# A picked expert's gate placed behind the next dot product, and GpSimd's query-weight remainders in four pieces

## The chip, the cores and the metric

The kernel runs on one core of a Trainium2 chip. The metric is the device time of one execution in microseconds (us). The kernel before takes 1302.95 us, the median of three runs (1302.8, 1302.95 and 1305.87). The engines are PE (TensorE), PEld (its weight loads), DVE (VectorE), ACT (ScalarE), POOL (GpSimd) and SP (SyncE, which only issues transfers).

## The reference

One step of a hybrid decoder: 256 prompt tokens with 16 meta tokens ahead of them and 8 × 8 tokens of running sequences pass a mixer (convolution and state-space branches) and then a layer of product-key experts. The change touches only the second half. 320 tokens are computed there, with 16384 experts of width 1024:

```python
def peer_block(xb, w_q, keys, U, V):
    q = (xb @ w_q).reshape(T, PEER_HEADS, 2, D_KEY // 2)
    s = jnp.einsum('thcd,hckd->thck', q, keys)
    s1, i1 = lax.top_k(s[:, :, 0], PEER_TOPK)
    s2, i2 = lax.top_k(s[:, :, 1], PEER_TOPK)
    ...
    ids = i1[f // 16] * N_KEYS + i2[f % 16]
    g = jax.nn.softmax(sc, axis=-1)
    act = jax.nn.gelu(jnp.einsum('thkd,td->thk', U[ids], xb))
    w = g * act
    return jnp.einsum('thk,thkd->td', w, V[ids])
```

Each token picks 16 experts in each of 8 heads. An expert's row of U gives, by a dot product with the token, its activation; a Gelu and the softmax weight make the gate; the gate scales the expert's row of V, and the 128 scaled rows are summed.

## The kernel before

**Up to 534 us** runs the mixer. The change leaves it as it is.

**Query weights (534 to 612 us, with the last of their products beyond).** Sixteen weights of 128 columns (j = 0 to 15) are loaded by SP. Each is split in a high part `wh`, rounded by ScalarE, and a low part `wl`, the remainder, computed by GpSimd (`split`, L244). The three products ah·wh, al·wh and ah·wl are summed on TensorE (L176), ScalarE copies the result out (`qT`, L1185), and TensorE multiplies it with the keys (`psc`, L1189). DVE then finds the 16 best keys (`top16`). In the loop stand also the preparations of the experts: at j = 4 the tokens' inputs, at j = `EXTRA` − 4 and j = `EXTRA` those of eight tokens apart (`x2e`, `acce`; the transposes `px`). At j = 7 the first four heads of the first 128 tokens are through: `heads_tasks(0)` computes their expert numbers `gid`, and `ahead(0)` issues the first gathers.

**Two ways to an expert's sum.** 128 tokens, and eight more in a second table, are *gathered*: 136 columns of picks (`NCOL`), each a column of 128 picks, one for each partition. The other 184 tokens (`ND`) are *dense*: for all 16384 experts, in 128 blocks, TensorE multiplies a block of U with the tokens (u-blocks, L1411), ScalarE takes the Gelu into S (L1413), S is multiplied by a table of the picked weights (`g_step`, L1435 to L1450, 23 for each half of the experts), and TensorE multiplies with the blocks of V (v-blocks, L1513). A block is 512 KB (`eraw`), is issued by SP or, for every odd one, by ScalarE (L1394), and lies in a ring of eight buffers.

**A column** is four steps: GpSimd gathers 128 rows of U and V side by side, 1 MB (`wuv`, five buffers, L1143); DVE forms 128 dot products (L1299, into `scg`); ScalarE applies Gelu (L1301) and the softmax weight (L1304); DVE adds gate times V row to `ygat` or `acce` (L1309). `pick_row(n)` emits, in this order, the gather of column n + 3 (`DEEP` = 4, the row's own column counted), dot n, Gelu and gate of n, and sum n − 1. A gather also waits for the block that lies `LEAD` = 4 steps back at that time. After the 64th v-block the distance is `NEAR` = 2 in place of `DEEP`.

**What sets the order.** A `Feed` hands out rows, the remaining top-16 tasks and the g_steps evenly between blocks: 45 rows in 84 u-blocks, 26 in the next 44 (with 23 g_steps), 35 in 64 v-blocks (with 23 g_steps), and the rest in the 61 blocks up to block 126, after which `finish` ends the gathered tokens and `finish_dense` the dense ones. Within this a scheduler orders each engine's instructions; a dependency marked `NoSync` orders without a wait in the hardware, one marked `Sync` waits. Each engine works strictly in its order, its transfers' issues included.

Of the kernel before, what the change touches and what calls it, by code (L numbers as in the profile page):

```python
# [7 lines left out]
F32 = mybir.dt.float32  # L8
# [6 lines left out]
OP = mybir.AluOpType  # L15
AX = mybir.AxisListType

D = 1024
# [24 lines left out]
NPICK = 128  # L43
NCOL = NPICK + (NPICK // XQ if NX else 0)
XAT = 64
HG = 4
EXTRA = 7
LEAD = 4
GT = 8
NP = 2  # L50
# [14 lines left out]
LATE = 24  # L65
OH = 2
UV = 5
DEEP = 4
NEAR = 2
GLAG = 12  # L70
XRES = 104
# [87 lines left out]
def body(tc, ia, oa, stop=None):  # L159
    nc = tc.nc  # L160
    with ExitStack() as top:
# [77 lines left out]
            nc.vector.tensor_tensor(v, v, t, op=OP.mult)  # L239
            nc.vector.scalar_tensor_tensor(dst, v, 1.5, t, op0=OP.add, op1=OP.mult)  # L240

        def split(h, l, src, on_pool=False, on_dve=False):
            (nc.vector.tensor_copy if on_dve else nc.scalar.copy)(h, src)  # L243
            (nc.gpsimd if on_pool else nc.vector).tensor_tensor(l, src, h.bitcast(F32), op=OP.subtract)  # L244

        def stack3(dst, src, n, pool, tag):
            w_ = src.shape[-1]
# [19 lines left out]
        def weight(src, i):  # L267
            raw = wp.tile([128, KD, 128], F32, name="wraw", bufs=rb[0])
            nc.sync.dma_start(raw, src[i].rearrange("p (k m) -> p k m", m=128))
            h = wp.tile([128, KD, 128], F32R, name="wh", bufs=2)  # L270
            l = wp.tile([128, KD, 128], F32R, name="wl", bufs=2)
            nw[0] += 1
            f_ = lm[0]
            on_dve = int((nw[0] + 1) * f_) > int(nw[0] * f_)
            split(h, l, raw, on_pool=not on_dve, on_dve=lm[0] == 1)
            return h, l

        lm, nw = [LM[3]], [NW0]
# [135 lines left out]
        def project(i, xs_=xn, name="pj"):  # L414
            if ready:
                return ready.pop(0)
            w = weight(ia["w_in"], i)
            pf = ps.tile([128, PJ], F32, name=name, tag="pj", bufs=3)
            proj(pf[:, :T if xs_ is xn else T2], w, xs_)
            return pf  # L420
# [503 lines left out]
        for j in range(KD):  # L924
# [5 lines left out]
            for s in range(2):  # L930
                w = weight(ia["w_mo"], 2 * j + s)
                proj(p, w, lambda k: tuple(yg[4 * s + k // 2][c_][:, k % 2, :] for c_ in range(2)),
                     first=(s == 0), last=(s == 1))
# [3 lines left out]
        for j in range(KD):  # L937
            w = weight(ia["w_o"], j)
# [6 lines left out]
                                           op0=OP.mult, op1=OP.subtract)  # L945
# [19 lines left out]
        x2m = gp.tile([NGAT, D], F32, name="x2m")  # L965
        gid = gp.tile([128, NCOL], I32, name="gid")
        ggw = gp.tile([128, NCOL], F32, name="ggw")
        scg = gp.tile([128, NCOL], F32, name="scg")
# [7 lines left out]
        if NX:  # L976
            x2e = gp.tile([128, D], F32, name="x2e")
# [28 lines left out]
        def expert_inputs():  # L1006
            nc.scalar.activation(x2m, ygat, AF.Copy, scale=rsT[:, 0:1])
            nc.gpsimd.tensor_tensor(x2m, x2m, n2r, op=OP.mult)
            for k in range(KD):
                nc.scalar.activation(nd[:, k], xT[:, k, NGAT:NGAT + ND], AF.Copy, scale=V("n2", k))  # L1010
                if k % 2:
                    nk = nd[:, k - 1:k + 1]
                    nc.gpsimd.tensor_tensor(nk, nk, rs2[:, None, NGAT:NGAT + ND].to_broadcast([128, 2, ND]), op=OP.mult)
# [3 lines left out]
        def extra_copies():  # L1017
            E0 = NGAT + ND
            x_ = gp.tile([128, 2 * D], F32, name="wuv", bufs=UV)[:, :(KD + 1) * 128].rearrange("p (k c) -> p k c", c=128)
            xes.append(x_)  # L1020
            v_ = x_.rearrange("p k (q t) -> p k q t", t=NX)
            nc.vector.tensor_copy(v_[:, KD], rs2[:, None, E0:T2].to_broadcast([128, XQ, NX]))
            nc.vector.tensor_copy(v_[:, :KD], xT[:, :, None, E0:T2].to_broadcast([128, KD, XQ, NX]))

        def extra_tokens():
            nc.gpsimd.memset(acce, 0.0)
            xe = xes[0][:, KD]
            p = misc([128, 4], "prs")
            nc.tensor.matmul(p[:, 3:4], xe, ident[:, 0:1], start=True, stop=True)
            nc.scalar.copy(rsT[:, 3:4], p[:, 3:4])  # L1030
            for c_ in range(2):
                p = misc([128, 512], "px")
                cs = slice(c_ * 512, c_ * 512 + 512)
                for k in range(4):
                    nc.tensor.transpose(p[:, k * 128:(k + 1) * 128], xes[0][:, 4 * c_ + k], ident)
                nc.scalar.copy(acce[:NX, cs], p[:NX])
                nc.scalar.activation(x2e[:, cs], p, AF.Copy, scale=rsT[:, 3:4])
                nc.gpsimd.tensor_tensor(x2e[:, cs], x2e[:, cs], n2r[:, cs], op=OP.mult)
# [97 lines left out]
        COLS = list(range(XAT)) + list(range(NPICK, NCOL)) + list(range(XAT, NPICK))  # L1136
# [15 lines left out]
        def ahead(n):  # L1152
            for i_ in range(n, min(n + (DEEP if len(vstep) <= HB else NEAR), NCOL)):
                if i_ not in pend:
                    pend[i_] = gather(COLS[i_])
# [20 lines left out]
        for j in range(16):  # L1176
# [4 lines left out]
            w = weight(ia["w_q"], j)  # L1181
# [5 lines left out]
            for i, (t0, L) in enumerate(KTILES):  # L1187
                n, up = 2 * heads_of[i], 64 * (j // (2 * heads_of[i]))
                nc.tensor.matmul(p[:, i], qT[:, t0 - up:t0 - up + 128], keys[:, j, :], start=True, stop=True)  # L1189
                s_ = sall[i][:, j % n] if i else kp.tile([128, NK], F32, name="sco", bufs=9)  # L1190
                scored = nc.scalar.copy(s_[up:up + L], p[up:up + L, i]).ins.name
                if i == 0:
                    top16(sv[i], si[i], s_[:L], j)
            if j == 4:
                expert_inputs()
            if j == EXTRA - 4:
                extra_copies()
            if j == EXTRA:
                extra_tokens()
# [7 lines left out]
        parts = [(0, SA), (SA, SB), (SB, 128)]  # L1207
# [87 lines left out]
        def pick_dot(n):  # L1295
            ahead(n)
            c, u = COLS[n], pend[n]
            w = scg[:, c:c + 1]
            nc.vector.scalar_tensor_tensor(u[:, :D], u[:, :D], 1.0, x2m if c < NPICK else x2e,  # L1299
                                           op0=OP.mult, op1=OP.mult, accum_out=w)  # L1300
            i_ = nc.scalar.activation(w, w, AF.Gelu)  # L1301
            tc.add_manual_dep(i_.ins, scored, mybir.DependencyInfo(mybir.DependencyClass.NoSync,
                                                                   mybir.DependencyReason.DATA), reason="scores first")
            nc.scalar.activation(w, w, AF.Copy, scale=ggw[:, c:c + 1])  # L1304

        def pick_sum(n):
            c, u = COLS[n], pend.pop(n)
            a_ = ygat if c < NPICK else acce
            nc.vector.scalar_tensor_tensor(a_, u[:, D:], scg[:, c:c + 1], a_, op0=OP.mult, op1=OP.add)  # L1309

        def group_sum():
            for c_ in range(2):
                p = misc([128, 512], "pgo")
                cs = slice(c_ * 512, c_ * 512 + 512)
                after(nc.tensor.matmul(p[:NX], C(f"sel{NX}"), acce[:, cs], start=True, stop=True), vstep[-1])
                nc.scalar.copy(x2e[:NX, cs], p[:NX])

        def pick_row(n):
            if NX and n == XAT - 9:
                extra_columns()  # L1320
            if n < NCOL:
                pick_dot(n)
            if n:
                pick_sum(n - 1)
            if NX and n == NCOL - GLAG:
                group_sum()

        ops = [(2.6, lambda n=n: pick_row(n)) for n in range(NCOL + 1)]

        def take(n):  # L1330
            t = ops[:n]
# [317 lines left out]
```

## Time and profile before

| | us |
|---|---|
| median of the runs | 1302.95 |
| the profiled execution | 1309.37 |
| its span in the profile | 1307.6 |
| query weights, scores, first picks | 534 to 612 |
| u-blocks 0 to 83, with the columns from 644 on | 612 to 785 |
| u-blocks 84 to 127, with g_steps | 785 to 960 |
| v-blocks | 960 to 1294 |
| finish of the dense tokens | 1294.8 to the end |

The profiled execution lasts 6.4 us longer than the median of the runs, so times of the trace are compared with this execution, and the difference between two states of the kernel is carried over to the median. A busy share that belongs to the whole span says little here, since the stages have different limits; the tables by stage and the waits of each engine are the views to read. In a waits table a row reads: engine, tile and line that waited, what released it, us in total, times, longest.

### The profile page before, as it was taken

The numbers are of one execution on the slowest core, as the hardware profiler recorded it, in microseconds if no ns is written. First come the engines' busy times: TensorE is split into PE (matmuls) and PEld (weight loads), VectorE is DVE, ScalarE is ACT, GpSimd is POOL, SyncE is SP. The second block draws the span as 40 slices with busy tenths as digits, with TensorE's granted clock in tenths as the row PEclk, the third lists the DMA queues.
The fourth block names the chain that finished last, engine by engine and source line by source line (L and its number), as shares of the span: only waits on it lengthen the run. The fifth ranks groups of instructions, "written<-read, shape, count | busy, mean of one in ns | idle before, by whom it ended". The sixth has DMA issues, their size and how long they took to land.

```text
span 1307.6 us, 23843 instructions
## 1 busy us (share of the span) xinstructions
PE 1274.4 (97%) x9015; PEld 1224.2 (94%) x9015; DVE 966.3 (74%) x2240; ACT 525.5 (40%) x1395; POOL 587.1 (45%) x504
## 2 busy tenths in 40 slices
PE   9999999999989999999998999999999999999997
PEld 7899989999879999999998999989999999999997
DVE  7978779878887235649998967788787887544444
ACT  6688777888766444534222221122211110101102
POOL 2487777877774666854042222223323322122210
PEclk9899999999999999999999999999999999999999
DMA  6434453454433444765889999999999999999992
GB/s 249 151 128 175 169 190 134 154 186 164 150 127 136 145 146 147 255 235 206 331 328 415 416 413 415 414 412 409 415 415 415 414 415 415 387 416 415 413 412 104
DMA packets 85907, 373.80 MB, mean 286 GB/s; under 512 B 10000, under 2 KB 15376, under 8 KB 66208
## 3 DMA queue, kind: packets, MB, share of 16 engines
q1 hardware_dynamic: 48336, 166.82, 34.5%
q0 software_dynamic: 19584, 142.62, 26.7%
q10 hardware_dynamic: 17872, 62.84, 12.1%
q8 instruction: 71, 1.16, 0.4%
q14 instruction: 44, 0.36, 0.1%
HBM read 359.18 MB, written 13.06 MB: 285 GB/s over the span
## 4 chain that ended last, share of the span: by engine, by line
PE 73%; DVE 13%; DMA 10%; ACT 2%; POOL 1%; issue 1%; DVEq 0%; ACTq 0%; POOLq 0%
PE pj L176 30%; PE va L1513 24%; PE pj L1411 10%; DMA wuv<-in_peer_uv_dram,gid 9%; DVE ygat L1309 2%; DVE pcv L505 1%; PE pg L1439 1%; PE pst L176 1%; DVE wuv L1299 1%; PE pdec L176 1%; PE po L176 1%; PE py L176 1%; DMA eraw<-in_uT_dram 1%; PE pq L176 1%; DVE pj L519 1%
## 5 line engine op out<-in xcount | busy, mean ns | idle before, releaser
L1143 POOL DMA_INDIRECT wuv<-in_peer_uv_dram,gid x136 | 176.7, 1299 | 485.7 <-PE va L1513 127.6
L244 POOL TENSOR_TENSOR wl<-wraw,wh 128x1024 fp32r<-128x1024 f32 x112 | 270.1, 2414 | 126.3 <-ACT wh L243 65.8
L1513 PE MATMUL va<-S,eraw 128*128 128x184 f32 x2048 | 325.4, 320 | 0.0
L1513 PEld LDWEIGHTS va<-S,eraw 128*128 128x128 f32 x2048 | 318.9, 190 | 0.9 <-issue 0.9
L1411 PE MATMUL pj<-nd,eraw 128*128 128x184 f32 x1792 | 293.9, 323 | 10.4 <-DMA eraw<-in_uT_dram 7.2
L1411 PEld LDWEIGHTS pj<-nd,eraw 128*128 128x128 f32 x1792 | 281.9, 192 | 12.4 <-issue 8.2
L176 PE MATMUL pj<-ah,wh 128*128 128x336 f32 (+1 forms) x768 | 243.9, 328 | 0.4 <-ACT xnf L219 0.4
L176 PE MATMUL pj<-al,wh 128*128 128x336 f32 (+1 forms) x768 | 233.5, 317 | 0.0
L1309 DVE SCALAR_TENSOR_TENSOR ygat<-wuv,scg,ygat 128x1024 f32<-128x1024 f32 x128 | 163.8, 1280 | 92.2 <-ACT scg L1304 92.2
L1301 ACT ACTIVATE scg<-scg 128x1 f32<-128x1 f32 x136 | 27.2, 202 | 455.4 <-DVE wuv L1299 326.4
L1299 DVE SCALAR_TENSOR_TENSOR wuv<-wuv,x2m 128x1024 f32<-128x1024 f32 x128 | 156.1, 1220 | 52.7 <-DMA wuv<-in_peer_uv_dram,gid 52.4
L243 ACT CAST wh<-wraw 128x1024 fp32r<-128x1024 f32 x125 | 131.0, 1049 | 80.4 <-PE pj L176 47.7
L505 DVE SCALAR_TENSOR_TENSOR pcv<-ccat,vec,pcv 128x256 f32<-128x256 f32 x464 | 149.0, 381 | 17.1 <-ACT pcv L503 17.1
L176 PEld LDWEIGHTS pj<-ah,wh 128*128 128x128 f32 x768 | 146.6, 191 | 6.2 <-issue 2.0
L176 PEld LDWEIGHTS pj<-al,wh 128*128 128x128 f32 x768 | 146.3, 191 | 0.9
L176 PE MATMUL pj<-ah,wl 128*128 128x336 f32 (+1 forms) x768 | 136.3, 315 | 0.7 <-POOL wl L244 0.7
L176 PEld LDWEIGHTS pj<-ah,wl 128*128 128x128 f32 x768 | 120.0, 189 | 1.2 <-POOL wl L244 1.0
L1413 ACT ACTIVATE S<-pj 128x184 f32<-128x184 f32 x128 | 37.4, 314 | 79.2 <-PE pj L1411 79.0
L519 DVE SCALAR_TENSOR_TENSOR pj<-mcat,vec,pj 128x360 f32<-128x360 f32 x96 | 56.4, 589 | 0.0
L219 ACT ACT_TABLE_LOAD x38 | 48.8, 1283 | 0.6
L1450 DVE SCALAR_TENSOR_TENSOR S<-pg,S 128x232 f32<-128x232 f32 (+1 forms) x92 | 34.5, 417 | 12.7 <-PE pg L1439 12.7
L1304 ACT ACTIVATE scg<-scg,ggw 128x1 f32<-128x1 f32 x136 | 39.7, 294 | 4.5 <-ACT scg L1301 0.2
(386 smaller groups left out, 1700.6 us busy)
## 6 DMA issues: line engine op xcount, KB each, us to landing
wraw<-in_w_in_dram SPq DMA_DIRECT2D x80, 512.0 KB, 4.3
eraw<-in_vE_dram SPq DMA_DIRECT2D x64, 512.0 KB, 10.2
eraw<-in_vE_dram ACTq DMA_DIRECT2D x64, 512.0 KB, 10.1
eraw<-in_uT_dram SPq DMA_DIRECT2D x60, 512.0 KB, 9.9
eraw<-in_uT_dram ACTq DMA_DIRECT2D x52, 512.0 KB, 10.0
st<-in_state_dram SPq DMA_DIRECT2D x8, 1024.0 KB, 6.9
out_ssm_s_dram<-st SPq DMA_DIRECT2D x8, 1024.0 KB, 6.3
wraw<-in_w_mo_dram SPq DMA_DIRECT2D x16, 512.0 KB, 3.2
```

Source lines behind the costliest of these rows:

```text
L176: i_ = nc.tensor.matmul(*a_, **kw)
L219: i_ = nc.scalar.activation(out, in_, f, **kw)
L243: (nc.vector.tensor_copy if on_dve else nc.scalar.copy)(h, src)
L244: (nc.gpsimd if on_pool else nc.vector).tensor_tensor(l, src, h.bitcast(F32), op=OP.subtract)
L505: t = nc.vector.scalar_tensor_tensor(o, i_, wv, a_, op0=OP.mult, op1=OP.add)
L519: nc.vector.scalar_tensor_tensor(o, cat[:, w:w + n], wv, o, op0=OP.mult, op1=OP.add)
L1143: i_ = nc.gpsimd.indirect_dma_start(out=u, out_offset=None, in_=ia["peer_uv"], in_offset=bass.IndirectOffsetOnAxis(ap=gid[:, c:c + 1], axi ...
L1299: nc.vector.scalar_tensor_tensor(u[:, :D], u[:, :D], 1.0, x2m if c < NPICK else x2e, op0=OP.mult, op1=OP.mult, accum_out=w)
L1304: nc.scalar.activation(w, w, AF.Copy, scale=ggw[:, c:c + 1])
L1309: nc.vector.scalar_tensor_tensor(a_, u[:, D:], scg[:, c:c + 1], a_, op0=OP.mult, op1=OP.add)
L1411: i_ = nc.tensor.matmul(p[:, :ND], raw[:, k, :], nd[:, k, :], start=(k == 0), stop=(k == KD - 1))
L1513: i_ = nc.tensor.matmul(va[k // 2][:, k % 2], raw[:, k, :], Sv(b), start=(b == 0 and k % 2 == 0), stop=(b == 127), skip_group_check=True)
```

## The change

Four edits, three of them to the columns and the first picks:

- `pick_row(n)` now emits dot n, then Gelu and gate of column n − 1, then sum n − 2. The Gelu of n − 1 is ordered behind dot n by a `NoSync` dependency ("rank"). There is one row more (`NCOL` + 2).
- `DEEP` is 3 and not 4, so row n emits the gather of column n + 2.
- `EXTRA` is 5 and not 7: the copies for the eight tokens apart come at j = 1 and not 3, their transposes and products at j = 5 and not 7.
- GpSimd's low part of each of the sixteen query weights is computed in four instructions of 128 x 256 and not in one of 128 x 1024. Other weights are split as before.

```diff
--- before.py
+++ after.py
@@ -44,7 +44,7 @@
 NCOL = NPICK + (NPICK // XQ if NX else 0)
 XAT = 64
 HG = 4
-EXTRA = 7
+EXTRA = 5
 LEAD = 4
 GT = 8
 NP = 2
@@ -65,7 +65,7 @@
 LATE = 24
 OH = 2
 UV = 5
-DEEP = 4
+DEEP = 3
 NEAR = 2
 GLAG = 12
 XRES = 104
@@ -239,9 +239,13 @@
             nc.vector.tensor_tensor(v, v, t, op=OP.mult)
             nc.vector.scalar_tensor_tensor(dst, v, 1.5, t, op0=OP.add, op1=OP.mult)
 
-        def split(h, l, src, on_pool=False, on_dve=False):
+        def split(h, l, src, on_pool=False, on_dve=False, parts=1):
             (nc.vector.tensor_copy if on_dve else nc.scalar.copy)(h, src)
-            (nc.gpsimd if on_pool else nc.vector).tensor_tensor(l, src, h.bitcast(F32), op=OP.subtract)
+            n = src.shape[1]
+            m = n // parts if on_pool and len(src.shape) == 3 else n
+            for q in range(0, n, m):
+                (nc.gpsimd if on_pool else nc.vector).tensor_tensor(l[:, q:q + m], src[:, q:q + m],
+                                                                    h[:, q:q + m].bitcast(F32), op=OP.subtract)
 
         def stack3(dst, src, n, pool, tag):
             w_ = src.shape[-1]
@@ -272,7 +276,7 @@
             nw[0] += 1
             f_ = lm[0]
             on_dve = int((nw[0] + 1) * f_) > int(nw[0] * f_)
-            split(h, l, raw, on_pool=not on_dve, on_dve=lm[0] == 1)
+            split(h, l, raw, on_pool=not on_dve, on_dve=lm[0] == 1, parts=1 if lm[0] else 4)
             return h, l
 
         lm, nw = [LM[3]], [NW0]
@@ -1295,12 +1299,18 @@
         def pick_dot(n):
             ahead(n)
             c, u = COLS[n], pend[n]
+            i_ = nc.vector.scalar_tensor_tensor(u[:, :D], u[:, :D], 1.0, x2m if c < NPICK else x2e,
+                                                op0=OP.mult, op1=OP.mult, accum_out=scg[:, c:c + 1])
+            return i_.ins.name
+
+        def pick_gate(n, behind):
+            c = COLS[n]
             w = scg[:, c:c + 1]
-            nc.vector.scalar_tensor_tensor(u[:, :D], u[:, :D], 1.0, x2m if c < NPICK else x2e,
-                                           op0=OP.mult, op1=OP.mult, accum_out=w)
             i_ = nc.scalar.activation(w, w, AF.Gelu)
-            tc.add_manual_dep(i_.ins, scored, mybir.DependencyInfo(mybir.DependencyClass.NoSync,
-                                                                   mybir.DependencyReason.DATA), reason="scores first")
+            for name in (scored, behind):
+                if name:
+                    tc.add_manual_dep(i_.ins, name, mybir.DependencyInfo(mybir.DependencyClass.NoSync,
+                                                                         mybir.DependencyReason.DATA), reason="rank")
             nc.scalar.activation(w, w, AF.Copy, scale=ggw[:, c:c + 1])
 
         def pick_sum(n):
@@ -1318,14 +1328,15 @@
         def pick_row(n):
             if NX and n == XAT - 9:
                 extra_columns()
-            if n < NCOL:
-                pick_dot(n)
-            if n:
-                pick_sum(n - 1)
+            behind = pick_dot(n) if n < NCOL else None
+            if 0 < n <= NCOL:
+                pick_gate(n - 1, behind)
+            if n > 1:
+                pick_sum(n - 2)
             if NX and n == NCOL - GLAG:
                 group_sum()
 
-        ops = [(2.6, lambda n=n: pick_row(n)) for n in range(NCOL + 1)]
+        ops = [(2.6, lambda n=n: pick_row(n)) for n in range(NCOL + 2)]
 
         def take(n):
             t = ops[:n]
```

Most lines of the changed kernel have other numbers: L244 is L247, L1143 is L1147, L1189 is L1193, L1299 is L1302, L1301 is L1309, L1304 is L1314, L1309 is L1319, L1394 is L1405, L1411 is L1422, L1413 is L1424, L1439 is L1450, L1450 is L1461.

On DVE, among the u-blocks with g_steps, the rows of before are these (L1299 is a dot, L1309 a sum; the number behind `wuv` tells the columns apart):

```order
L1309 SCALAR_TENSOR_TENSOR ygat_6624<-wuv_8761,scg_6628,ygat_6624 128x1024
L1299 SCALAR_TENSOR_TENSOR wuv_8779,scg_6628<-wuv_8779,x2m_6625 128x1024
L1435 TENSOR_TENSOR oh_9316<-oh_9316,gT_6631 128x512 x2
L1309 SCALAR_TENSOR_TENSOR ygat_6624<-wuv_8779,scg_6628,ygat_6624 128x1024
L1299 SCALAR_TENSOR_TENSOR wuv_8797,scg_6628<-wuv_8797,x2m_6625 128x1024
L1309 SCALAR_TENSOR_TENSOR ygat_6624<-wuv_8797,scg_6628,ygat_6624 128x1024
L1299 SCALAR_TENSOR_TENSOR wuv_8815,scg_6628<-wuv_8815,x2m_6625 128x1024
```

And of the changed kernel, at a like place (L1302 is a dot, L1319 a sum):

```order
L1446 TENSOR_TENSOR oh_9509<-oh_9509,gT_6631 128x512 x2
L1302 SCALAR_TENSOR_TENSOR wuv_8876,scg_6628<-wuv_8876,x2m_6625 128x1024
L1319 SCALAR_TENSOR_TENSOR ygat_6624<-wuv_8858,scg_6628,ygat_6624 128x1024
L1302 SCALAR_TENSOR_TENSOR wuv_8936,scg_6628<-wuv_8936,x2m_6625 128x1024
L1319 SCALAR_TENSOR_TENSOR ygat_6624<-wuv_8876,scg_6628,ygat_6624 128x1024
L1461 SCALAR_TENSOR_TENSOR S0_7582<-pg_9460,S0_7582 128x29x8
```

The sum of a column stood right behind its own dot (column 8797), and now stands behind the dot of the next column (8876 behind 8936), so a column's buffer is held for one row more. This holds for the whole program.

On TensorE the scores of j = 7 for the first 128 tokens are what `gid` waits for last. The rows of before around them (`qT_6682` in the last row is that of j = 7; the other `psc` rows belong to its neighbours):

```order
L176 MATMUL pj<-ah,wl 128x320 x2
L1189 MATMUL psc<-keys,qT_6681 128x128
L1189 MATMUL psc<-keys,qT_6683 128x128
L176 MATMUL pj<-ah,wl 128x320 x6
L1189 MATMUL psc<-keys,qT_6681 128x128
L1189 MATMUL psc<-keys,qT_6682 128x128
```

And of the changed kernel (the first `qT_6682` is that of j = 7):

```order
L176 MATMUL pj<-ah,wh 128x320
L176 MATMUL pj<-al,wh 128x320
L176 MATMUL pj<-ah,wl 128x320 x8
L1193 MATMUL psc<-keys,qT_6682 128x128
L1193 MATMUL psc<-keys,qT_6681 128x128
L1193 MATMUL psc<-keys,qT_6682 128x128
L1193 MATMUL psc<-keys,qT_6681 128x128
```

Counted from the first query product, 264 products stood ahead of these scores and now 288 do, a whole weight's 24 more; the eight transposes `px` of the eight tokens apart stood behind them and now stand ahead. On DVE 63 instructions stood between these scores and `gid` and now 70 do, and between `gid` and the first sum 113 small instructions beside five dots and now 96 beside five.

On GpSimd the rows of before from the tokens' inputs to the gathers (L244 is a low part, L1038 the inputs of the eight tokens apart, L1143 the gathers):

```order
L1008 TENSOR_TENSOR x2m<-x2m,wuv 128x1024
L244 TENSOR_TENSOR wl<-wraw,wh 128x1024 x9
L1038 TENSOR_TENSOR x2e<-x2e,wuv 128x512 x2
L244 TENSOR_TENSOR wl<-wraw,wh 128x1024
L1143 DMA wuv<-in_peer_uv_dram,gid 128x2048 x136
```

And of the changed kernel:

```order
L1012 TENSOR_TENSOR x2m<-x2m,wuv 128x1024
L247 TENSOR_TENSOR wl<-wraw,wh 128x256 x28
L1042 TENSOR_TENSOR x2e<-x2e,wuv 128x512
L247 TENSOR_TENSOR wl<-wraw,wh 128x256 x4
L1042 TENSOR_TENSOR x2e<-x2e,wuv 128x512
L247 TENSOR_TENSOR wl<-wraw,wh 128x256 x12
L1147 DMA wuv<-in_peer_uv_dram,gid 128x2048 x136
```

A weight's low part is four rows where it was one, and the inputs of the eight tokens apart stand before the last four and three weights, where they stood before the last one.

## The prediction

> **What bounds the kernel now.** The page's first part, then the busy time by stage, then TensorE's waits. In a stage row stand its start and end, its length, the busy time of PE, PEld, DVE, ACT and POOL, TensorE's granted clock, the DMA share and GB/s.
>
> ```profile
> PE 1274.4 (97%) x9015; PEld 1224.2 (94%) x9015; DVE 966.3 (74%) x2240; ACT 525.5 (40%) x1395; POOL 587.1 (45%) x504
> ```
> ```profile
> 534.00:612.00 78.00, 76.97 (x531) 75.19 (x530) 51.38 (x206) 36.66 (x90) 46.38 (x24) 1.00 0.65 228
> 612.00:645.00 33.00, 33.00 (x220) 33.00 (x219) 32.33 (x183) 9.81 (x39) 4.18 (x5) 1.00 0.93 357
> 645.00:683.00 38.00, 37.86 (x244) 37.58 (x243) 38.00 (x117) 8.88 (x28) 15.30 (x10) 1.00 0.83 303
> 683.00:785.00 102.00, 94.98 (x613) 93.23 (x612) 85.84 (x206) 25.18 (x89) 28.49 (x23) 0.98 1.02 415
> 785.00:880.00 95.00, 88.63 (x698) 86.31 (x697) 75.54 (x133) 17.31 (x71) 23.77 (x20) 0.98 1.02 414
> 880.00:960.00 80.00, 80.00 (x636) 79.07 (x635) 66.07 (x119) 16.86 (x64) 28.17 (x18) 1.00 1.02 412
> 960.00:1120.00 160.00, 160.00 (x1313) 158.60 (x1312) 130.53 (x228) 17.19 (x69) 44.20 (x34) 1.00 1.02 415
> ```
> ```profile
> PE pj L1411 <- DMA eraw<-in_uT_dram: 7.2, 4, 3.3
> PE pj L1411 <- ACT scg L1301: 3.1, 1, 3.1
> PE pg L1439 <- DVE oh L1435: 2.6, 2, 2.2
> ```
>
> TensorE sets the time. Nothing that the change touches runs before 534 us. From 880 to 1120 TensorE is busy throughout, and nothing can be gained there. Between 683 and 880 it is idle for 102.00 − 94.98 + 95.00 − 88.63 = 13.4 us. That is the whole budget for a gain, with the clock of 0.98 beside it (0.02 × 197 = 3.9 us at most). The waits name 12.9 us of it. In the same stages DVE is busy 85.84 of 102 us, and the DMA engines move 415 GB/s at a share of 1.02, so they are full as well.
>
> The next rows are the timeline at the second wait (start, duration, engine and line; the bracket is the idle time before).
>
> ```profile
> 693.42 0.20 ACT L1301 ACTIVATE scg<-scg 128x1 f32<-128x1 f32 x1 [3.92 <-DVE wuv L1299]
> 693.77 0.34 ACTq L1394 DMA_DIRECT2D eraw<-in_uT_dram  x1
> 697.78 1.22 DVE L1299 SCALAR_TENSOR_TENSOR wuv<-wuv,x2m 128x1024 f32<-128x1024 f32 x1 [1.12 <-DMA wuv<-in_peer_uv_dram,gid]
> 699.04 0.20 ACT L1301 ACTIVATE scg<-scg 128x1 f32<-128x1 f32 x1 [4.57 <-DVE wuv L1299]
> 699.31 21.85 PE L1411 MATMUL pj<-nd,eraw 128*128 128x184 f32 x128 [3.08 <-ACT scg L1301]
> ```
>
> ScalarE works in order. The Gelu of a column stands in its queue right after the row's block, and waits there for a dot product that DVE has not begun, here because the gather has not landed (1.12 us). Behind it stand the eviction of a finished u-block (L1413), which TensorE needs for its PSUM, and the issue of every second block load. TensorE lost 3.08 us to the eviction. The loads are the second price:
>
> ```profile
> 681.18 0.20 ACT L1301 ACTIVATE scg<-scg 128x1 f32<-128x1 f32 x1 [2.20 <-DVE wuv L1299]
> 681.43 0.33 ACTq L1394 DMA_DIRECT2D eraw<-in_uT_dram  x1
> 691.00 5.22 PE L1411 MATMUL pj<-nd,eraw 128*128 128x184 f32 x32 [2.10 <-DMA eraw<-in_uT_dram]
> 733.63 0.20 ACT L1301 ACTIVATE scg<-scg 128x1 f32<-128x1 f32 x1 [5.70 <-DVE wuv L1299]
> 733.87 0.34 ACTq L1394 DMA_DIRECT2D eraw<-in_uT_dram  x1
> 743.57 0.71 PE L1411 MATMUL pj<-nd,eraw 128*128 128x184 f32 x3 [0.95 <-DMA eraw<-in_uT_dram]
> 791.29 9.04 SPq L1288 DMA_DIRECT2D xigd<-xig  x4
> 819.08 4.24 PE L1411 MATMUL pj<-nd,eraw 128*128 128x184 f32 x16 [3.26 <-DMA eraw<-in_uT_dram]
> ```
>
> Twice a load issued by ScalarE right after such a wait lands 9.6 and 9.7 us later, at the moment at which TensorE's wait ends. The last of the four waits, 3.26 us, comes after SP's queue was held for 9.04 us by other transfers; ScalarE has no part in it.
>
> **The gate behind the next dot.** These rows are ScalarE's waits between 680 and 880, VectorE's waits for the gate in the whole run, and the gathers from issue to landing.
>
> ```profile
> ACT scg L1301 <- DVE wuv L1299: 140.4, 41, 5.7
> DVE ygat L1309 <- ACT scg L1304: 92.2, 67, 6.1
> wuv<-in_peer_uv_dram,gid POOLq DMA_INDIRECT x136, 17.0
> ```
>
> After the change the Gelu of column n−1 is asked for when dot n is next on DVE, and its own dot was done a whole column earlier. It is kept behind dot n in the scheduler's order, which is no wait on DVE in the hardware, so it runs at once. Most of the 140.4 us of ScalarE's waiting goes. What TensorE has of that: the eviction stall, −3.1 us; and the load stalls at 691 and 743 and the third one of the four, together 7.2 − 3.3 = −3.9 us. The second is bounded by 0 (the DMA engines are full, and an earlier issue only queues longer) and by 3.9; I take 3.9, since the two rows show landing 9.6 to 9.7 us after issue in the full stage itself. The 3.3 us at 819 stays. No instruction is added on ScalarE; it has the same two per column, and it is busy only 25.18 of 102 us.
>
> DVE gains also: the sum no longer waits for the gate (92.2 us in 67 waits). DVE is not on TensorE's path in these stages but for 2.6 us, so its worth lies between 0 and 2.6; I take 0, because the two waits at pg are bursts of work on DVE, not gates.
>
> What is late next: the buffer of a column comes free one row later, and the gathers go out three columns ahead and not four. A gather also waits for a block four steps back. At 84/45 = 1.87 blocks per row, a gather before has 3 × 1.87 + 4 = 9.6 blocks from its release to its dot, and now 2 × 1.87 + 4 = 7.7 blocks. A block is 21.85/8 = 2.73 us, so that is 26 us before and 21 us now, against 17.0 us to landing. It still fits, with 4 us to spare where there were 9. One gather less in flight is 1.05 MB, which at 415 GB/s is 2.5 us of DMA time that the block loads have sooner. That makes between −2.5 us (all of it falls on stalled loads) and +6 us (the third rival); I take 0, nearest the landing time, as the load stalls are already counted as gone.
>
> The Trainium skill, "DMA: Bandwidth & Descriptors", section "Queues, rings and completion order", says that each DMA engine takes turns between the queues that have work, a packet at a time. By that rule the gathers' share does not depend on how many of them wait, as long as one does, and the 2.5 us would be nothing. No row of the trace splits the share by queue over so short a stretch, so I keep 0 by the rows alone.
>
> **The start of the columns.** The order of the change shows the scores that the first 64 picks wait for after 24 more products and 8 transposes on TensorE, and 7 more small instructions on DVE from there to the gather indices; but 17 fewer small instructions between the indices and the first sum. The rows: the time of the indices and of the first sum, one small instruction, and the instructions that GpSimd's low parts hold up. Of these there are four between 595 and 602; the first is gh, the last pab; together they take 7.36 us and in the same forms at 737 to 740 together 1.29.
>
> ```profile
> 610.81 0.18 DVE L1120 CAST gid<-idh 128x64 int32<-128x64 f32 x1
> 644.60 1.18 DVE ygat L1309
> L1050 DVE FIND_INDEX8 si<-sv,sall 128x8 uint32<-128x128 f32 x24 | 6.7, 284 | 0.0
> 595.95 1.95 DVE L1122 TENSOR_TENSOR gh<-cv 128x64 f32<-128x64 f32 x1
> 601.14 2.38 DVE L1086 TENSOR_TENSOR pab<-pab,plo 128x64 bf16<-128x64 bf16 x1
> 600.63 2.81 POOL L244 TENSOR_TENSOR wl<-wraw,wh 128x1024 fp32r<-128x1024 f32 x1
> 737.20 0.20 DVE L1122 TENSOR_TENSOR gh<-cv 128x64 f32<-128x64 f32 x1
> 739.93 0.22 DVE L1086 TENSOR_TENSOR pab<-pab,plo 128x64 bf16<-128x64 bf16 x1
> L674 POOL TENSOR_TENSOR st<-st,el 128x256 f32<-128x256 f32 x64 | 37.9, 630 | 0.0
> L244 POOL TENSOR_TENSOR wl<-wraw,wh 128x1024 fp32r<-128x1024 f32 x112 | 270.1, 2414 | 126.3 <-ACT wh L243 65.8
> ```
>
> A product takes 33.00/220 = 0.15 us, so TensorE brings those scores 32 × 0.15 = 4.8 us later, and DVE adds 7 × 0.284 = 2.0. A small DVE instruction that met a low part ended with it (601.14 + 2.38 beside 600.63 + 2.81). With quarters of 0.63 us it waits a quarter at most: the 7.36 − 1.29 = 6.1 us lost shrink to 4 × 0.63 = 2.5, a gain of 3.6. The Trainium skill, "SBUF — State Buffer", section "SBUF: two separate sides", calls this port pair an exclusive lock that GpSimd or DVE holds for a whole instruction; by that rule four quarters back to back could win the lock again each time, and the gain would lie anywhere between 0 and 6.1 us. The indices come 4.8 + 2.0 − 3.6 = 3.2 us later, the first sum 17 × 0.284 = 4.8 us sooner than that: 1.6 us sooner than before, bounds −4.1 and +2.0 by the port waits. TensorE is busy throughout 612 to 683 whatever the columns do, so this is worth only what the DMA engines are ahead by at 683, when they are at 303 to 357 GB/s and later full: 0 to −1.6. I take 0.
>
> GpSimd itself: 64 × 0.63 = 40.3 us for 16 × 2.41 = 38.6, so +1.7 us over a stage in which it is idle 78 − 46.38 = 31.6 us. Cost 0; without that cover, 1.7.
>
> **The end.** The last columns go by the 61 blocks after the 64th; there is one row more to hand out, and the finishing of the picked tokens follows the last sum.
>
> ```profile
> 1288.04 2.42 DVE L1507 SCALAR_TENSOR_TENSOR wraw<-x2e,frs,wuv 128x512 f32<-128x512 f32 x2
> 1294.76 0.32 ACT L1525 ACTIVATE sqd<-va 128x184 f32<-128x184 f32 x1 [6.66 <-PE va L1513]
> ```
>
> It ends at 1290.5, 4.3 us ahead of TensorE's last products. A column without the gate's wait comes sooner, if anything. Cost 0; a second dot's time, 1.2, would still fit.
>
> **Sum.** −3.1 − 3.9 = −7.0 us against the profiled execution, 1309.37 us with a span of 1307.6, so 1302.4. That execution is 6.4 us above the median; I take the difference over to the median: 1302.95 − 7.0 = 1296.0.
>
> **Rivals.** First, everything idle goes: the whole 13.4 us, so 1289.6, and 1285.7 with the clock. For it speaks that ScalarE's waits were at every second block; against it the stall behind SP's transfers and the two at pg. Second, the DMA engines are the bound: at 415 GB/s a load issued sooner lands no sooner, and only the gather less in flight helps, 1302.95 − 2.5 = 1300.5. For it speaks the share of 1.02 through all the stages, against it that TensorE runs without a wait from 880 on at the same share. Third, slower: the gather has 21 us, and where it takes longer than that, dot n stands waiting at the head of DVE's in-order queue, with sum n−1 and its buffer and the one-hot (oh) of the next g_step behind it, and TensorE waits at pg. One such wait shows in this run:
>
> ```profile
> 878.00 0.95 PE L1439 MATMUL pg<-oh 128*128 128x64 f16 x16 [2.20 <-DVE oh L1435]
> ```
>
> At 2.2 us apiece, five of the 46 g_steps (23 for each half of the experts) undo the gain and reach +0.3%, and six give 6 × 2.2 − 7.0 = +6.2, so 1309. It decides from a mean landing of about 21 us; the 17.0 shown speaks against it. Since fewer gathers share the engines, it should rather fall.
>
> **Chances.** The forecast (1293 to 1299) 0.43, all the idle time 0.13, the DMA engines as the bound 0.26, slower 0.18. A measurement of this kernel tells 0.3%, 3.9 us, from no change. So faster 0.56, the same 0.26, slower 0.18. The range leaves about a fourth of the first rival and a third of the third out: 1288 to 1309. It takes in the bounds above, −7.0 − 2.5 − 1.6 = −11 and +6.
>
> **What would show it.** Right: ScalarE's waits for the dot (L1301 before) fall to a few us, DVE's for the gate to none, TensorE has no wait on the gate's line, and 3 to 4 us for block loads, the one behind SP's transfers; the indices come at about 614 and the first sum at about 643; no small DVE instruction beside a low part takes over 0.9 us; the gathers land in 17 us or less. Wrong: DVE's waits for gathers (52 us in the run) grow, TensorE's waits at pg grow past 2.6 us, or the idle time between 683 and 880 stays near 13 us under other names.

## The result and the profile after

The changed kernel is slower: 1320.29 us median of four runs (1319.77 to 1323.95) against 1304.41 (1302.8 to 1307.79), a ratio of 1.0128 with a 95% interval of 1.0111 to 1.0145. The forecast was 1296.0, within 1288 to 1309. The profiled execution lasted 1320.37 us, its span is 1318.6, so 11.0 us over the span of before. That is less than the 15.9 us between the medians, because the profiled execution of before lies 5.0 us above its median and this one at it.

The stages of the changed kernel, in the columns of the table by stage shown above, and TensorE's waits from 540 us on:

```profile
683.00:785.00 102.00, 97.88 (x654) 95.85 (x653) 87.08 (x215) 25.16 (x86) 21.90 (x21) 1.00 1.02 414
785.00:880.00 95.00, 90.28 (x721) 88.64 (x720) 68.27 (x125) 16.99 (x64) 17.23 (x16) 0.96 0.98 380
880.00:960.00 80.00, 80.00 (x635) 79.00 (x634) 60.27 (x110) 14.78 (x56) 17.60 (x15) 1.00 0.99 383
960.00:1120.00 160.00, 160.00 (x1289) 158.78 (x1288) 120.39 (x212) 14.81 (x60) 31.52 (x31) 1.00 1.00 393
```
```profile
PE prd L1537 <- ACT sqd L1536: 21.0, 1, 21.0
PE pj L1422 <- DMA eraw<-in_uT_dram: 7.4, 4, 4.7
PE pj L1422 <- ACT S L1424: 1.4, 2, 1.0
```

A part of the gain that was forecast is there: between 683 and 880 TensorE is idle for 4.12 + 4.72 = 8.8 us where it was 13.4. What is new is one wait of 21.0 us at the very end, and DMA engines that move less between 785 and 1120 (380 to 393 GB/s for 412 to 415 before). The timeline at the end shows the wait:

```profile
1224.42 60.00 PE L1524 MATMUL va<-S,eraw 128*128 128x184 f32 x384
1296.23 2.68 DVE L1319 SCALAR_TENSOR_TENSOR ygat<-wuv,scg,ygat 128x1024 f32<-128x1024 f32 x2
1305.05 0.32 ACT L1536 ACTIVATE sqd<-va 128x184 f32<-128x184 f32 x1 [1.63 <-DVE wraw L1518]
1305.43 5.02 PE L1537 MATMUL prd<-sqd,cst 128*128 128x184 f32 x16 [21.00 <-ACT sqd L1536]
```

TensorE ends its last v-block at 1284.4. The last sum of the gathered tokens ends only at 1298.9, their finish stands behind it on DVE and ScalarE, and the finish of the dense tokens behind that. The same 384 products before:

```profile
1236.59 60.00 PE L1513 MATMUL va<-S,eraw 128*128 128x184 f32 x384
```

They ended at 1296.6, and ScalarE was waiting for them. So the end costs (1318.6 − 1284.4) − (1307.6 − 1296.6) = 23.2 us more, and TensorE's way to it is 12.2 us shorter. Of these 12.2 the mixer, which the change does not touch, has 4.3, by the same products in both executions:

```profile
508.82 1.33 PE L176 MATMUL pj<-mh,wl 128*128 128x320 f32 x8
```
```profile
504.52 1.33 PE L176 MATMUL pj<-mh,wl 128*128 128x320 f32 x8
```

The first row is before, the second after. That leaves 7.9 us of gain on TensorE's way, and 23.2 − 7.9 − 4.3 = 11.0, the difference of the spans. Without the mixer's 4.3 it would be 15.3, close to the 15.9 between the medians.

The columns were late. The next rows count the sums (L1309, L1319) by stage; the number behind DVE's busy time is their count. Before:

```profile
785.00:960.00 175.00, 46.21 (x37) 0.99 1.02 413
960.00:1120.00 160.00, 43.58 (x34) 1.00 1.02 415
1265.00:1300.00 35.00, 5.14 (x4) 1.00 0.48 191
```

After:

```profile
785.00:960.00 175.00, 39.12 (x32) 0.98 0.99 381
960.00:1120.00 160.00, 39.67 (x31) 1.00 1.00 393
1265.00:1300.00 35.00, 16.66 (x13) 0.83 0.84 338
```

There are eight sums fewer between 785 and 1120, and 13 after 1265 where there were 4. One column shows what it went through. Before, column 48, first GpSimd's row of its gather and of the gather five columns on, then DVE's dot and sum:

```profile
832.60 0.94 POOL L1143 DMA_INDIRECT wuv<-in_peer_uv_dram,gid  x1 [1.84 <-issue]
...
856.47 0.94 POOL L1143 DMA_INDIRECT wuv<-in_peer_uv_dram,gid  x1 [1.84 <-PE pj L1411]
```
```profile
852.59 1.22 DVE L1299 SCALAR_TENSOR_TENSOR wuv<-wuv,x2m 128x1024 f32<-128x1024 f32 x1
...
854.42 1.28 DVE L1309 SCALAR_TENSOR_TENSOR ygat<-wuv,scg,ygat 128x1024 f32<-128x1024 f32 x1 [0.60 <-ACT scg L1304]
```

After, column 52, the same rows, and ScalarE's at its Gelu:

```profile
866.40 0.94 POOL L1147 DMA_INDIRECT wuv<-in_peer_uv_dram,gid  x1 [1.93 <-DVE ygat L1319]
...
896.99 0.94 POOL L1147 DMA_INDIRECT wuv<-in_peer_uv_dram,gid  x1 [7.77 <-PE pg L1450]
```
```profile
884.32 1.22 DVE L1302 SCALAR_TENSOR_TENSOR wuv<-wuv,x2m 128x1024 f32<-128x1024 f32 x1
...
890.91 1.22 DVE L1302 SCALAR_TENSOR_TENSOR wuv<-wuv,x2m 128x1024 f32<-128x1024 f32 x1
...
894.95 1.28 DVE L1319 SCALAR_TENSOR_TENSOR ygat<-wuv,scg,ygat 128x1024 f32<-128x1024 f32 x1 [2.80 <-ACT scg L1314]
```
```profile
894.00 0.32 ACT L1424 ACTIVATE S<-pj 128x184 f32<-128x184 f32 x1 [2.58 <-PE pj L1422]
894.00 0.33 ACTq L1405 DMA_DIRECT2D eraw<-in_uT_dram  x1
894.38 0.20 ACT L1309 ACTIVATE scg<-scg 128x1 f32<-128x1 f32 x1
```

Before, the sum starts 1.8 us after the dot. After, the dot starts at 884.32, the next dot at 890.91, the Gelu behind an eviction at 894.38 and the sum at 894.95, 10.6 us after its dot. Only then is the buffer free, and the gather five columns on is issued 2.0 us later. The buffer was held for 28.6 us and not 21.8. With five buffers a column takes (hold + 2.0)/5. The means over columns 40 to 63, from the start of the gather to the start of the sum, are all worked out from the trace. The last column counts the sums that stand in DVE's order ahead of the end of the 24th g_step (the first among the v-blocks) and of the 46th, the last:

| kernel | buffers | tie | hold, us | (hold + 2.0)/buffers | measured, us per column | sums ahead of g_step 24 / 46 |
|---|---|---|---|---|---|---|
| before | 5 | no | 22.0 | 4.8 | 4.85 | 71 / 105 |
| changed | 5 | yes | 26.3 | 5.7 | 5.45 | 63 / 92 |
| before, four buffers (e7) | 4 | no | 20.7 | 5.7 | 5.68 | 62 / 90 |
| changed, room for six, five used (e5) | 5 | yes | 25.1 | 5.4 | 5.43 | 63 / 92 |
| changed, six buffers (e6) | 6 | yes | 26.0 | 4.7 | 4.66 | 71 / 103 |

The kernel before makes a sum every 4.7 us here (175 us for 37 sums), and in all five rows a gather goes out as soon as a buffer is free (2.0 us after the sum begins, 2.3 in e6), so even the kernel before ran at the edge of its buffers. While that is so, the rule and the measured time must agree, and differ only by where the stretch is cut: the rule says what a column takes, not why the hold is long.

The landings in the trace say more. In the changed kernel the 26.3 us are 9.8 from issue to landing, 9.0 in which the landed rows lie, and 7.5 from the dot to the sum. No dot of columns 40 to 95 starts less than 4.4 us after its rows have landed. Before, the dot of columns 40 to 63 follows the landing by 1.2 us on average (18 of the 24 landings are on record), and the sum follows the dot by 2.7. DVE's waits for gathers between 785 and 1120 us, before and then after:

```profile
DVE wuv L1299 <- DMA wuv<-in_peer_uv_dram,gid: 26.4, 26, 1.9
```
```profile
DVE wuv L1302 <- DMA wuv<-in_peer_uv_dram,gid: 2.6, 1, 2.6
```

So in this stretch of the changed kernel a gather that went out sooner would have brought no dot forward. The columns go at the pace of the built order, which is fixed before the kernel runs: by the 24th g_step eight sums, and by the last one thirteen, had been put behind where they stood before. The tie and the number of buffers act on that order, as the table shows. That the scheduler counts the hold of a buffer as the rule does is likely, and not shown.

### The profile page after: what moved, and what is told of

Read it like the earlier page. It is cut to its first block, busy times and chain, and to the rows that moved or that the text cites. A ratio compares the mean times of both kernels' runs of the same rounds, so it can differ in the third digit from the quotient of the medians.

```text
span 1318.6 us, 23876 instructions
## 1 busy us (share of the span) xinstructions
PE 1271.4 (96%) x9015; PEld 1222.8 (93%) x9015; DVE 956.1 (73%) x2240; ACT 527.4 (40%) x1395; POOL 571.8 (43%) x552
## 4 chain that ended last, share of the span: by engine, by line
PE 76%; DVE 10%; DMA 9%; ACT 2%; issue 1%; POOL 1%; ACTq 0%; DVEq 0%; SPq 0%; POOLq 0%
PE pj L176 31%; PE va L1524 23%; PE pj L1422 13%; DMA wuv<-in_peer_uv_dram,gid 5%; DMA eraw<-in_uT_dram 3%; DVE ygat L1319 2%; PE pg L1450 1%; PE pst L176 1%; DVE wuv L1302 1%; PE po L176 1%; PE pdec L176 1%; PE py L176 1%; DVE pcv L509 1%; DMA wdt<-in_w_dt_dram 1%; PE pq L176 1%
## 5 line engine op out<-in xcount | busy, mean ns | idle before, releaser
L1147 POOL DMA_INDIRECT wuv<-in_peer_uv_dram,gid x136 | 151.5, 1114 | 537.8 <-PE va L1524 212.8
L247 POOL TENSOR_TENSOR wl<-wraw,wh 128x1024 fp32r<-128x1024 f32 (+1 forms) x160 | 280.3, 1766 | 117.1 <-ACT wh L243 68.9
L1422 PE MATMUL pj<-nd,eraw 128*128 128x184 f32 x1792 | 293.6, 323 | 8.8 <-DMA eraw<-in_uT_dram 7.4
L1422 PEld LDWEIGHTS pj<-nd,eraw 128*128 128x128 f32 x1792 | 280.9, 191 | 10.7 <-issue 8.4
L1319 DVE SCALAR_TENSOR_TENSOR ygat<-wuv,scg,ygat 128x1024 f32<-128x1024 f32 x128 | 164.0, 1281 | 99.5 <-ACT scg L1314 99.2
L1302 DVE SCALAR_TENSOR_TENSOR wuv<-wuv,x2m 128x1024 f32<-128x1024 f32 x128 | 156.0, 1218 | 30.3 <-DMA wuv<-in_peer_uv_dram,gid 28.8
L1309 ACT ACTIVATE scg<-scg 128x1 f32<-128x1 f32 x136 | 26.9, 200 | 366.3 <-PE va L1524 198.6
L1424 ACT ACTIVATE S<-pj 128x184 f32<-128x184 f32 x128 | 39.2, 320 | 179.2 <-PE pj L1422 171.9
L1461 DVE SCALAR_TENSOR_TENSOR S<-pg,S 128x232 f32<-128x232 f32 (+1 forms) x92 | 34.7, 419 | 53.8 <-PE pg L1450 53.8
L1314 ACT ACTIVATE scg<-scg,ggw 128x1 f32<-128x1 f32 x136 | 39.8, 294 | 8.6 <-PE va L1524 4.4
```

The lines of the kernel that those rows point to most:

```text
L247: (nc.gpsimd if on_pool else nc.vector).tensor_tensor(l[:, q:q + m], src[:, q:q + m], h[:, q:q + m].bitcast(F32), op=OP.subtract)
L1147: i_ = nc.gpsimd.indirect_dma_start(out=u, out_offset=None, in_=ia["peer_uv"], in_offset=bass.IndirectOffsetOnAxis(ap=gid[:, c:c + 1], axi ...
L1302: i_ = nc.vector.scalar_tensor_tensor(u[:, :D], u[:, :D], 1.0, x2m if c < NPICK else x2e, op0=OP.mult, op1=OP.mult, accum_out=scg[:, c:c + 1])
L1422: i_ = nc.tensor.matmul(p[:, :ND], raw[:, k, :], nd[:, k, :], start=(k == 0), stop=(k == KD - 1))
```

## The experiments

The theories. **Q**: the Gelu's place behind block loads on ScalarE is the cause. **B**: the sum behind the next dot holds a buffer for one column more, and five buffers don't carry it. **D**: gathers three ahead are too late. **W**: the query weights' part is to blame.

**e1, the columns' part alone.**

```diff
-EXTRA = 5
+EXTRA = 7
-split(..., parts=1 if lm[0] else 4)
+split(..., parts=1)
```

> The changed kernel with the query weights' low parts whole again and EXTRA at 7: only the columns' new order is left, with the gathers three ahead. Theory Q (queue): tying a column's Gelu behind the next dot moves it behind more block loads in ScalarE's fixed order, 12 Gelus come after the last block load here (13 in the changed kernel, 2 in the one before), each column holds its buffer for about 28 us instead of 21, and the columns end after TensorE; so 1317 to 1322 us, with TensorE waiting some 20 us for the finish. Theory D (depth): the gathers are issued too late because they are three ahead and not four; the same 1317 to 1322. Theory W (query weights): the first picks are to blame; then this is 1300 to 1306.

Measured: 1325.97 us, ratio 1.016 (1.0126 to 1.0194), 4 us above the range expected; TensorE waits 21.2 us at the end. W falls. The loss is larger than that of the whole change.

**e2, the query weights' part alone** (on the kernel before: `EXTRA = 5`, low parts in four).

> The kernel before with the low parts in quarters and EXTRA at 5 alone. Theories Q and D: no column is later, so 1300 to 1305 us; the gather indices come 3 to 6 us earlier than in the kernel before, as in the profile of the changed kernel, and nothing ends later. Theory W: 1315 to 1321.

Measured: 1304.64, ratio 0.9992 (0.9973 to 1.001), no difference. The indices came at 610.33 with the mixer at the time of before, so half a microsecond earlier and not 3 to 6: that part of the expectation missed.

**e3, without the tie.**

```diff
-            for name in (scored, behind):
+            for name in (scored,):
```

> The changed kernel without the tie of the Gelu behind the next dot; the gathers stay three ahead, the sums are still asked for two rows later, the quarters stay. Theory Q: ScalarE's order is that of before again (one Gelu after the last block load), so 1298 to 1306 us, and ScalarE waits over 300 us for dots as before. Theory D: the distance is what counts, so 1315 to 1321.

Measured: 1301.82, ratio 0.9973 (0.9954 to 0.9992), if anything faster than before. D falls, and with it the sums asked for two rows later: without the tie there is no loss. One Gelu stands behind the last block load in ScalarE's order, as was expected, and 70 and 104 sums stand ahead of the 24th and the 46th g_step.

**e4, the V loads by SP.**

```diff
-(nc.scalar if i % 2 and (name == "vE" or i > LATE) else nc.sync)
+(nc.scalar if i % 2 and name != "vE" and i > LATE else nc.sync)
```

> The changed kernel with all V block loads issued by SP, none by ScalarE: the gates stay tied behind the next dot, but in the v-blocks no block load stands ahead of them on ScalarE. Theory Q: from 960 us on the sums wait only for the gate itself (dot to sum falls from about 10.7 us to 5 or 6), a column holds its buffer 23 to 25 us, the columns catch up a part of their 30 to 40 us, and the end is 1300 to 1312 us. Theory D: the loads' queue does not matter, 1317 to 1322.

Measured: 1329.22, ratio 1.0181 (1.0147 to 1.0216). Two new waits make it hard to read, TensorE's for V blocks from one queue and ScalarE's for the eight tokens' sums, behind which the gates stood:

```profile
PE va L1524 <- DMA eraw<-in_vE_dram: 26.2, 26, 1.1
```
```profile
ACT x2e L1326 <- PE pgo L1325: 48.7, 2, 48.5
```

The time lies outside both ranges. From 954 to 1118 us (columns 64 to 95), before the gates met ScalarE's long wait, each Gelu ran right after its own dot, with no block load ahead of it. Still the hold was 24.2 us (24.5 in the changed kernel), and the dots of columns 64 to 91 all started 1.2 us later than in the changed kernel, so none came sooner. That speaks against Q, and was the ground for B; it also shows once more that the built order sets the pace.

**e5 and e6, room for a sixth buffer, and the buffer.** The room comes from less prefetch, fewer score buffers and one one-hot buffer; e6 has `UV = 6` beside it.

```diff
-PRE = 4
-AGAIN = 24
-OH = 2
+PRE = 3
+AGAIN = 20
+OH = 1
...
-name="sco", bufs=9
+name="sco", bufs=5
...
-name="frs", bufs=2
+name="frs", bufs=1
```

> The changed kernel with room made for one more column buffer that is not yet used: three blocks prefetched at a time and not four, five score buffers and not nine, one one-hot buffer and not two. It is the control of the next run. Twelve or thirteen Gelus still come after the last block load in ScalarE's order, so both theories expect 1318 to 1330 us.

> The control with six column buffers; the tie stays. Theory B (buffers): a sum that must stand behind the next dot leaves only four of the five buffers for gathers on the way, and the time of a column is (hold + 2 us)/buffers: (26.3 + 2.0)/5 = 5.6 us in the changed kernel among the g_steps, where 4.85 is needed. With six it is 4.7, the columns keep up (2 Gelus after the last block load in ScalarE's order, as before), and the time is 15 to 25 us under the control, 1296 to 1306. Theory Q (the gates' place behind block loads on ScalarE by itself): the gates still stand a row later, so the gain is under 8 us.

Measured: e5 1319.81 (ratio 1.0121, 1.0103 to 1.014), e6 1299.48 (0.9962, 0.9947 to 0.9977). One buffer, the tie in place, is worth 20.3 us. Q is out as a cause by itself: the Gelus still stand a row later (5.9 us from dot to sum in columns 40 to 63), and 2 are behind the last block load. B is right about the hold and the number of buffers; but in e5, as in the changed kernel, DVE hardly waits for gathers between 785 and 1120 (0.2 us; 35.0 in e6), so the sixth buffer helps by the order that is built with it. The sums of e6 by stage answer to those above:

```profile
785.00:960.00 175.00, 48.26 (x38) 0.99 1.02 415
960.00:1120.00 160.00, 42.52 (x34) 1.00 1.02 414
1265.00:1300.00 35.00, 2.57 (x2) 0.92 0.29 109
```

**e7, the kernel before with one buffer less** (`UV = 4`, `DEEP = 3`).

> The kernel before with four column buffers and gathers three ahead, without any tie. Theory B: it shows the changed kernel's illness without its tie, a column every (22 + 2)/4 = 5.5 us or somewhat less as the gathers land sooner, 1315 to 1330 us, TensorE waiting 15 us or more for the finish. Theory Q: the Gelus stand ahead of the block loads as before, so 1302 to 1310.

Measured: 1334.45 us, ratio 1.0234 (1.0217 to 1.0251), 4 us above the range of B. There is no tie and the illness is the same: 32 sums between 785 and 960, DVE's waits for gathers between 785 and 1120 at 2.6 us, and at the end

```profile
PE prd L1526 <- ACT sqd L1525: 34.1, 2, 33.7
```

**e8, the tie in the first 84 u-blocks only.**

```diff
-            for name in (scored, behind):
+            for name in (scored, None if len(ustep) > SB else behind):
```

> The changed kernel with the tie only for rows among the first 84 u-blocks, where TensorE's stalls were, and none from there on. Both theories: TensorE keeps 3 to 6 us of the gain of the first u-blocks, the columns are 3 to 4 late at 785 us and catch up among the v-blocks (119 Gelus by the 48th V load on ScalarE, 118 before, 108 in the changed kernel), so 1294 to 1302 us.

Measured: 1304.35, ratio 0.9994 (0.9982 to 1.0007): the expectation missed. Between 683 and 785 TensorE was idle for 2.4 us only, as hoped, but the columns that were late then were caught up later (66 sums ahead of the 24th g_step, 102 ahead of the 46th), and between 1120 and 1265, at 415 GB/s, TensorE waited 5.0 us for V blocks. That fits bytes that were put off and had to be moved later; no run isolates it.

**e9 to e14, is the tie worth anything with six buffers?**

> The kernel with six column buffers (which ran at 1299.5 us) without the tie; nothing else differs. If the tie itself is worth what was forecast for it (ScalarE no longer held by a waiting gate, 5 to 7 us), this is 1303 to 1307. If the sixth buffer made that gain, it is 1297 to 1301, and the tie is worth nothing even where the buffers allow it.

> The kernel before with the room and six column buffers, gathers four ahead, no tie and whole low parts. If the tie is worth 5 to 7 us, 1302 to 1307, no better than before. If the sixth buffer is what counts, 1297 to 1301.

> The kernel with six column buffers and the tie, gathers four ahead in place of three. A gather already waits for its buffer or for the block four steps back, so both theories expect 1297 to 1302 us, the same as with three ahead.

> Six column buffers with the tie once more, now on one chip with the same kernel without the tie. If the tie is worth about 5 us where a sixth buffer carries it, this is 4 to 6 us below the run without it; if the two earlier calls differed by chance, they agree within 2 us.

> Six column buffers without the tie, the other half of the pair: 1302 to 1306 us, as in its first run.

> Six column buffers, the tie, gathers four ahead. It came out 4 us above the kernel with three ahead, which nothing had forecast. If that is real, it is 3 to 5 us above it here too; by my earlier reason, the same.

e9 is e6 without the tie, e10 the kernel before with the room and `UV = 6`, e11 is e6 with `DEEP = 4`. e12 to e14 are e6, e9 and e11 once more, on one chip.

| run | us | ratio to before | 95% interval |
|---|---|---|---|
| e9, six, no tie | 1304.43 | 1.0003 | 0.9989 to 1.0016 |
| e10, before, six | 1309.50 | 1.0042 | 1.0026 to 1.0057 |
| e11, six, tie, four ahead | 1303.55 | 0.9991 | 0.9981 to 1.0001 |
| e12, six, tie | 1300.35 | 0.9957 | 0.9945 to 0.9969 |
| e13, six, no tie | 1303.81 | 0.9982 | 0.9971 to 0.9994 |
| e14, six, tie, four ahead | 1302.17 | 0.9979 | 0.9967 to 0.999 |

On one chip the tie is worth 3.5 us with six buffers, where 4 to 6 were expected (the intervals lie just apart), and 5.0 between e6 and e9, which ran on two chips. A sixth buffer without the tie shows no gain. The tie does on ScalarE what was meant, as the rows of ScalarE's waits in e12 and then e13 show, and TensorE's idle time between 683 and 880 is 7.8 and 10.4 us:

```profile
ACT scg L1309 <- DVE wuv L1302: 131.5, 43, 6.3
```
```profile
ACT scg L1309 <- DVE wuv L1302: 235.3, 73, 7.5
```

Gathers four ahead came out 4.1 us slower (e11 and e6, on two chips), which nothing had forecast, and then 1.8 on one chip, where 3 to 5 were expected and the intervals overlap; so the size is open. In e14 TensorE waits longer for the one-hots than in e12, here in that order, but single profiles don't settle it:

```profile
PE pg L1450 <- DVE oh L1446: 7.8, 3, 5.4
```
```profile
PE pg L1450 <- DVE oh L1446: 5.3, 6, 1.3
```

e10, 2.5 us above its highest expectation, also goes four ahead, and lacks the query weights' part; what its room alone costs was not measured. **e12, 1300.35 us, is faster than both kernels.** It is not clearly apart from e3, five buffers without the tie, whose interval (0.9954 to 0.9992) overlaps with its own.

## Why the prediction was wrong, point by point

- **The gain on TensorE** came out near in size: −7.9 us for −7.0 forecast, 4.6 of it idle time between 683 and 880 and 0.9 between 534 and 683; the rest is not resolved. The nearness is luck, as its parts were other ones. The eviction stall fell from 3.1 to 1.4 us, now under the eviction's own name (`S`, L1424). The load stalls did not shrink by 3.9: they are 7.4 us for 7.2, of which 4.7 is the one behind SP's transfers (3.3 before), so the other three went from 3.9 to 2.7. In their place the 2.6 us at pg, which I took to stay, went to nothing. How much of it is the tie is not separated with five buffers: between 683 and 880 the profile of e2 has 10.7 us of idle time and that of e3 10.2, both without the tie, for 8.8 with it. With six buffers, where no bytes are put off, the tie's share is 3.5 to 5.0.
- **"It is kept behind dot n in the scheduler's order, ... so it runs at once"** failed, but is not by itself what the columns lost. The Gelu waits for its own dot only, but it stands in ScalarE's order behind everything that was put ahead of it, and there, at dot n+1, are evictions and block loads that wait for TensorE. In the order of ScalarE's instructions, which could be read before the run, 13 Gelus stand behind the last block load of the changed kernel, and 2 in the kernel before. ScalarE's wait for dots between 680 and 880, forecast to fall from 140.4 to a few us, is 41.6; waits behind TensorE's blocks grew from 117.1 to 198.6 in the run; and the sum's wait for the gate, forecast to vanish, grew from 92.2 to 99.2. The next rows are of the whole run, before and then after. In e4 the Gelus of columns 64 to 95 did run at once, and those columns were as late.

```profile
ACT scg L1301 <- PE va L1513: 117.1, 25, 9.4
ACT scg L1301 <- DVE wuv L1299: 326.4, 91, 11.8
```
```profile
ACT scg L1309 <- PE va L1524: 198.6, 35, 10.6
ACT scg L1309 <- DVE wuv L1302: 107.2, 40, 7.5
DVE ygat L1319 <- ACT scg L1314: 99.2, 34, 7.5
```

- **"What is late next"**, taken at 0, is the step that failed. I compared a gather's lead in blocks with its 17.0 us to landing, and found 4 us to spare. The landings kept that promise: the rows lay 9.0 us before their dot. What the term leaves out is the buffer that a row holds until its sum, and with it the order that is built for five buffers: 63 sums ahead of the 24th g_step and not 71, and 5.45 us per column and not 4.85. The numbers were in the profile of before: hold 22.0, five buffers, 4.85 us per column. A sum behind the next dot adds a column, 4.85 (dot to sum went from 2.7 to 7.5): (22.0 + 4.85 + 2.0)/5 = 5.8 us, an upper end, where 4.7 are needed to keep the place of before.
- **The third rival** had the side right and the mechanism wrong. It wanted landings over 21 us and waits at pg. The gathers landed sooner (a median of 10.5 us for 17.0) and TensorE had no wait at pg. TensorE never felt the late columns until the end, since nothing but the finish needs their sums.
- **"The end ... Cost 0"** failed with it: 13 sums behind 1265 us, 23.2 us more behind the last v-block. This is more than the whole loss, since TensorE's way to the end is shorter.
- **The first picks.** The indices came at 606.24 us; with the mixer's 4.3 taken off, 0.3 earlier than before, where 3.2 later was forecast. The first sum starts at 636.8, in the same way 3.4 earlier, where 1.6 was forecast. The port waits shrank more than I took: the four instructions now take 0.21, 0.46, 0.95 and 0.75, 2.4 us in all and 1.1 over their time elsewhere, where I took 2.5 over. So 5.0 us came back and not 3.6; what else made up the rest was not traced.

```profile
596.33 0.21 DVE L1126 TENSOR_TENSOR gh<-cv 128x64 f32<-128x64 f32 x1
596.72 0.46 DVE L1086 TENSOR_SCALAR plo<-ci 128x64 uint32<-128x64 uint32 x1
598.23 0.95 DVE L1095 TENSOR_TENSOR cand<-pab,iorep 128x1024 bf16<-128x1024 bf16 x1
599.10 0.75 DVE L1090 TENSOR_TENSOR pab<-pab,plo 128x64 bf16<-128x64 bf16 x1
...
606.24 0.20 DVE L1124 CAST gid<-idh 128x64 int32<-128x64 f32 x1
```

The Trainium skill, "SBUF — State Buffer", section "SBUF: two separate sides", has the port pair locked for a whole instruction; the excess of each of these, 0.01 to 0.53 us, is less than one quarter's 0.77 and so agrees with that, and the lock was not lost to the next quarter each time.

That this part is worth nothing by itself was right (e2). Where the columns are the bound it is worth something: e1, without it, is 5.7 us above the changed kernel, in two sets of runs whose intervals (1.0126 to 1.0194, and 1.0111 to 1.0145) overlap, so its size is open.

## What to carry to other kernels

A ring of buffers has a rate of its own: hold time plus reissue, over the number of buffers. Before an order is changed so that a buffer is let go later, work that out for before and after, and compare it with the pace at which the rows are handed out; a wait that is moved off one engine's queue can come back as hold time, as it did here. Then look in the trace whether the data lie landed before they are used: where they do, as in columns 40 to 95 here, it is the built order that sets the pace in the run, and an earlier transfer gains nothing. And count in the built order of every engine what stands behind the last instruction of the path that now sets the end.

## What the runs showed of the hardware that was not expected

GpSimd's low part of 128 x 256 takes 0.77 us in the changed kernel, where another instruction of that shape took 0.63: four quarters are 3.1 us for 2.43 of the whole. It shows no cost here, as GpSimd was busy for 55.13 of the 78 us between 534 and 612.

```profile
L247 POOL TENSOR_TENSOR wl<-wraw,wh 128x256 fp32r<-128x256 f32 x64 | 47.4, 774 | 15.9 <-ACT sall L1195 11.6 <-ACT wh L243 3.1 <-ACT qT L1189 1.1
```
